# Weight-block sums of two row products, made ahead beside the gate and up products and kept in DRAM

## The chip, the cores and the metric

The kernel runs on one core of a Trainium2 chip. The metric is the device time of one execution in microseconds (us).

## What is computed

One decoder layer on 1024 tokens of width 1024, all in float32. The parts that matter here:

```python
f = _swiglu(_rmsnorm(h, ffn1_pre_g), ffn1_w_gate, ffn1_w_up, ffn1_w_down)
h = h + 0.5 * _rmsnorm(f, ffn1_post_g)
z = _rmsnorm(h, mix_pre_g) @ w_in            # u | v | pool | gate a | gate b
...                                          # gated spatial and pooling mixers, projections
f = _swiglu(_rmsnorm(h, ffn2_pre_g), ffn2_w_gate, ffn2_w_up, ffn2_w_down)
h = h + 0.5 * _rmsnorm(f, ffn2_post_g)
gate = jax.nn.sigmoid(_rmsnorm(h, ple_pre_g) @ ple_w_gate)
h = h + _rmsnorm(gate * (p @ ple_w_proj), ple_post_g)
```

The hidden width of both FFNs is 2816.

## The kernel before

Every large product is made by a scheme of seven products of half-size blocks (p1, p2, p5, p6, p3, p7, p4, in this order, `ORDER`). Both operands are needed as blocks and as sums of blocks. Of the left operand (the tokens), class `Seven` keeps seven tiles `X`; of the right operand (the weights), each of the products needs one block or one sum: p1 takes block 11, p2 block 21, p3 block 22; p5 takes 11+12, p6 adds 22 to that, p7 takes 12+22, p4 takes 11+12+22+21. Each float32 operand is then split into a high part (a cast on ScalarE, L147) and the rest (a subtraction on VectorE, L148), and each product of two blocks is three matmuls (`mm3`, L155 to L157).

An FFN first makes the gate and up products (`ffn_hidden`): eleven column groups of seven products with two output tiles each, weights loaded three steps ahead. A finished group is spilled to DRAM with its sums (`spill`), and sums of blocks of the down weights for later are made beside it (`down_sums`, two loads, four sums on VectorE, four stores into `t_d`). Then `ffn_down` makes the down product. Its last step finishes the token tiles 4 to 7 one by one, and `closing` treats each: a square with a sum on ScalarE (L168), a multiplication by the gain (L718), a reciprocal root on GpSimd (L162, L163), the residual on VectorE (L730), again a square (L168) and a root (L162, L163), and the scaling of the normalised tile (L178, into a `raw` tile). TensorE transposes that tile (L232), and `feed` turns it into the left operands of the next product (L148, L207, L212 to L215). I call the time of these four tiles the passage.

Behind each passage stands a row product (class `Rows`: seven steps, four output tiles each): v after the first FFN, the gate of the layer's end after the second. TensorE meanwhile makes p1 and p2 of it, two tile products between one transpose and the next. Its weights are made one step ahead. Those of v and of the last gate are built from the blocks as they are needed (`from_blocks`): loads at L522, and for p5, p6, p7 and p4 sums on VectorE (`each`, L151), two of 128x1024 per step, on tiles of the pool `raw`, which has six buffers. The blocks 11, 12 and 22 stay in these buffers until p7 has used them. The same pool holds the residual input of each token tile (L725) and, at the end, the output tiles (L1185). The row product by `w_o` has its sums from DRAM already (`from_stored`).

Small pieces of work are queued in `Later` with a key (the lowest goes first) and a cost in us; after each tile product some credit is given and pieces are let out. A timeline model then orders the instructions of each engine, and each engine, SP with its DMA queue too, runs them strictly in that order. The pools are `raw` (6), `f` (11 tiles of 128x1024), `hf` (4 of 128x512) and PSUM (8 banks).

Of the kernel before, what the change touches and what calls it, by code (L numbers as in the profile page):

```python
# [13 lines left out]
P = 128  # L14
T = 1024
D = 1024
# [5 lines left out]
HT = 512  # L22
# [61 lines left out]
def layer_kernel(ctx: ExitStack, tc: tile.TileContext, a: dict, out: bass.AP):  # L84
    nc = tc.nc
    x, p = a["x"][0], a["p"][0, 0]
# [13 lines left out]
    later = Later()  # L100
# [4 lines left out]
    def wt(shape):  # L105

        return wtp.tile([P, *shape], FR, name="wt", tag="wt")

    def raw(shape, dt=F32):

        return rawp.tile([P, *shape], dt, name="raw", tag="raw")

    def full(shape=(D,), dt=F32):

        return fp.tile([P, *shape], dt, name="f", tag="f")
# [11 lines left out]
    def scratch(name, n, w=D):  # L127
        return [dr.tile([P, w], F32, name=f"{name}{i}", tag=f"{name}{i}") for i in range(n)]
# [3 lines left out]
    ga_d, gb_d, y_d = (dr.tile([P, KD, T], F32, name=s, tag=s) for s in ("ga_d", "gb_d", "y_d"))  # L132
    as_d, bs_d = (scratch(s, 7, KD // 2 * HT) for s in ("a_s", "b_s"))

    tw_d = {s: [scratch(f"{s}_t{h}", 4) for h in range(2)] for s in ("w_out_a", "w_out_b", "w_o")}
    ws_d = dr.tile([P, HT], F32, name="ws_d", tag="ws_d")
    sv_d = dr.tile([P, KD, T], F32, name="sv_d", tag="sv_d")
# [12 lines left out]
    def add(dst, u, v, e=nc.vector):  # L150
        e.tensor_tensor(dst, u, v, op=ALU.add)  # L151
# [37 lines left out]
    class Seven:  # L189
        def __init__(self):  # L190
            self.op, self.kept = [None] * 7, {}
            count[0] += 10
            self.base = count[0]
# [10 lines left out]
        def sums(self, k, cols, a11, a12, a21, a22, s1, us):  # L204


            nc.vector.tensor_tensor(s1, a22, a21, op=ALU.subtract)  # L207
            self.put(2, k, cols, s1)
            self.put(6, k, cols, a22)

            def others():
                nc.vector.scalar_tensor_tensor(s1, a11, -1.0, s1, op0=ALU.mult, op1=ALU.subtract)  # L212
                self.put(3, k, cols, s1)
                nc.vector.scalar_tensor_tensor(a12, a12, -1.0, s1, op0=ALU.mult, op1=ALU.subtract)
                nc.vector.tensor_tensor(a11, a11, a21, op=ALU.subtract)  # L215

            later.before(self.base + 3, 4 * us, others)
            later.before(self.base + 4, us, lambda: self.put(4, k, cols, a12))
            later.before(self.base + 5, us, lambda: self.put(5, k, cols, a11))
# [145 lines left out]
    def from_blocks(block, put):  # L365


        def each(u, v):
            for x, y in zip(u, v):
                add(x, x, y, nc.vector)  # L370

        def make(i, st, keep):
            name = ORDER[i][0]
            if name in ("p1", "p2"):
                b = block(i, 0)
                if keep[i]:
                    st[("11", "21")[i]] = b
                return put(b)
            if name == "p5":
                st["11"] = st.get("11") or block(0, 0)  # L380
                st["12"] = block(0, 1)
                each(st["11"], st["12"])
                return put(st["11"])
            if name == "p6":
                st["22"] = block(1, 1)
                each(st["11"], st["22"])
                return put(st["11"])
            if name == "p3":
                return put(st["22"])
            if name == "p7":  # L390
                each(st["12"], st["22"])
                return put(st["12"])
            each(st["11"], st.get("21") or block(1, 0))
            return put(st["11"])

        return make

    def from_stored(block, put, sums):


        def make(i, st, keep):
            where = {"p1": (0, 0), "p2": (1, 0), "p3": (1, 1)}
            name = ORDER[i][0]
            return put(block(*where[name]) if name in where else sums(("p5", "p6", "p7", "p4").index(name)))

        return make
# [97 lines left out]
        return [one(t) for t in range(4)]  # L504

    class Rows:
        def __init__(self, w, stored=None):

            state = {}

            def sums(j):
                out = [raw([2, HT]) for _ in range(2)]
                for h, t in enumerate(out):
                    nc.sync.dma_start(t, stored[h][j].rearrange("p (k f) -> p k f", k=2))
                return out

            def block(r, c):
                out = []
                for h in range(2):
                    t = raw([2, HT])  # L520
                    r0 = r * HT + h * 256
                    nc.sync.dma_start(t, w[r0:r0 + 256, c * HT:(c + 1) * HT].rearrange("(k p) f -> p k f", p=P))  # L522
                    out.append(t)
                return out

            def put(b):
                out = []
                for h in range(2):
                    o = wt([2, 2, HT])
                    split(o[:, 0], o[:, 1], b[h])  # L530
                    out.append(o)
                return out

            make = from_stored(block, put, sums) if stored else from_blocks(block, put)
            self.right = Right(lambda i: make(i, state, (False, False)), list(range(7)), 1)

        def run(self, left, outs, last):
# [21 lines left out]
    def spill(g, dst):  # L559


        def keep(i, src):
            nc.sync.dma_start(dst(i), src)

        def first():
            keep(0, g["11"])
            keep(1, g["12"])
            keep(6, g["22"])
            s1, s2 = half(), half()
            nc.vector.tensor_tensor(s1, g["22"], g["21"], op=ALU.subtract)  # L570
            keep(2, s1)
            nc.vector.scalar_tensor_tensor(s2, g["11"], -1.0, s1, op0=ALU.mult, op1=ALU.subtract)
            keep(3, s2)
            g["s2"] = s2

        def second():
            s3, s4 = half(), half()
            nc.vector.scalar_tensor_tensor(s4, g["12"], -1.0, g["s2"], op0=ALU.mult, op1=ALU.subtract)
            keep(4, s4)
            nc.vector.tensor_tensor(s3, g["11"], g["21"], op=ALU.subtract)  # L580
            keep(5, s3)

        later.add(0, 1.4, first)
        later.add(0, 1.4, second)
# [3 lines left out]
        wg, wu = (a[f"{s}_w_{n}"][0] for n in ("gate", "up"))  # L588
        return Columns(HC, lambda c: ((wg, c, c + HC), (wu, c, c + HC)), 2)

    def ffn_hidden(s, left, cols, last):
        wd = a[f"{s}_w_down"][0]
        hid = {}

        def down_sums(c):

            state = []

            def put(i, u, v):
                o = half()  # L600
                add(o, u, v)
                nc.sync.dma_start(t_d[s][i][:, c * HT:(c + 1) * HT], o)
                return o

            def first():
                w = []
                for b in range(2):
                    w.append(full((2, HT)))
                    r = (c + b * HC) * P
                    nc.sync.dma_start(w[b], wd[r:r + P, :].rearrange("p (j f) -> p j f", j=2))  # L610
                b11, b12, b21, b22 = (w[i][:, j, :] for i in range(2) for j in range(2))
                t2 = put(3, put(2, b11, b12), b22)
                state.append(lambda: (put(6, t2, b21), put(5, b12, b22)))

            later.add(90, 1.4, first)
            later.add(91, 1.4, lambda: state.pop()())

        def outs(c):
            g = hid[c] = {}
            _, places, others = packed()  # L620

            def gate(key, src):
                g[key] = places(key)
                nc.scalar.activation(g[key], src, AF.Silu)

            def up(key, src):
                nc.vector.tensor_tensor(g[key], g[key], src, op=ALU.mult)

            return [Out(gate, places), Out(up, others)]

        def after(c):
            spill(hid.pop(c), lambda i: s_d[s][i][:, c * HT:(c + 1) * HT])
            if c < HC - 1:
                down_sums(c)
            if c == HC - 2:
                down_sums(c + 1)
            if c == HC - 1:
                later.flush()

        cols.run(left, outs, after, lambda i: last() if i == 6 else None)  # L640
# [108 lines left out]
    w_in = a["w_in"][0]  # L749
    h1_cols = hidden_weights("ffn1")  # L750
# [53 lines left out]
    left = Seven()  # L804
# [66 lines left out]
        return steps  # L871

    down = down_weights("ffn1")
    ffn_hidden("ffn1", left, h1_cols, lambda: down.ahead(3))
    v_rows = Rows(w_in[:, D:2 * D])
    left = Seven()
    ffn_down(
        down, closing(4.0, lambda t: x[t * P:(t + 1) * P, :], h1_d, "ffn1_post_g", "mix_pre_g", left),
# [6 lines left out]
    v, sgu = {}, []  # L885
# [264 lines left out]
    h2_cols = hidden_weights("ffn2")  # L1150
    left = Seven()
# [3 lines left out]
    )  # L1155

    down = down_weights("ffn2")
    ffn_hidden("ffn2", left, h2_cols, lambda: down.ahead(3))
    ple_rows = Rows(a["ple_w_gate"][0])
    left = Seven()  # L1160
    ffn_down(
        down, closing(4.0, lambda t: h2_d[t], h3_d, "ffn2_post_g", "ple_pre_g", left),
# [60 lines left out]
```

## Time and profile before

| what | before |
|---|---|
| median of three runs | 2148.37 us (2146.13 to 2148.41) |
| the profiled execution | 2153.78 us |
| its span | 2151.7 us |
| TensorE busy | 2070.9 us (96%) |
| VectorE busy | 1472.0 us (68%) |
| ScalarE busy | 939.9 us (44%) |
| moved by DMA | 429.52 MB, mean 200 GB/s |

Times in the profile count from the span's start. The gate and up products of the first FFN lie at about 60 to 480 us, its passage at 690 to 730; those of the second FFN at 1440 to 1830, its passage at 2030 to 2070. The last gate's product follows to the end.

### The profile page before, as it was taken

How to read it: one execution, taken by the hardware profiler on the slowest of the kernel's cores; microseconds unless marked ns; L12 is line 12 of the kernel's file. 1: busy time of each engine (PE TensorE's matmuls, PEld its weight loads, DVE VectorE, ACT ScalarE, POOL GpSimd, SP SyncE). 2: the span in 40 equal slices, each digit the busy share in tenths (PEclk: the TensorE clock that was granted, in tenths of full speed). 3: DMA queues.
4: the chain of work that ended last, by engine and by line, in shares of the span. 5: the costliest groups of instructions: out<-in, count | busy, mean ns of one | idle time of the engine just before them, and what ended most of it. 6: DMA issues, size and time to landing. Idle time of an engine off the chain costs nothing. (4 is left out here: it accounts for less than half of the span.)

```text
span 2151.7 us, 25497 instructions
## 1 busy us (share of the span) xinstructions
PE 2070.9 (96%) x9228; PEld 1712.7 (80%) x9228; DVE 1472.0 (68%) x1773; ACT 939.9 (44%) x1360; POOL 141.0 (7%) x212
## 2 busy tenths in 40 slices
PE   7999999999999799999999999989999999999986
PEld 6888888888887688888787887778888888888765
DVE  6866666677566887567576758886666667545687
ACT  7533333344435543334455535643333334444553
POOL 2000000000021110000000002300000000002112
PEclk9999999999999899999999999999999999999988
DMA  8454545399768236445389986635454547764635
GB/s 287 128 171 157 176 142 184 129 340 384 298 221 320 69 100 193 158 142 177 128 282 340 324 233 204 195 112 188 146 186 136 172 149 272 231 197 175 225 118 195
DMA packets 301486, 429.52 MB, mean 200 GB/s; under 512 B 19888, under 2 KB 176560, under 8 KB 301360
## 3 DMA queue, kind: packets, MB, share of 16 engines
q1 hardware_dynamic: 300272, 425.80, 58.3%
q0 software_dynamic: 1088, 2.10, 0.6%
q8 instruction: 72, 1.18, 0.2%
q14 instruction: 54, 0.44, 0.1%
HBM read 290.72 MB, written 137.10 MB: 199 GB/s over the span
## 5 line engine op out<-in xcount | busy, mean ns | idle before, releaser
L155 PE MATMUL ps<-X,wt 128*128 128x512 f32 x1904 | 743.0, 391 | 4.1 <-DVE f L345 2.4
L156 PE MATMUL ps<-X,wt 128*128 128x512 f32 x1904 | 743.2, 390 | 0.9 <-DVE X L148 0.9
L157 PE MATMUL ps<-X,wt 128*128 128x512 f32 x1904 | 741.8, 390 | 0.0
L148 DVE TENSOR_TENSOR wt<-raw,wt 128x1024 fp32r<-128x1024 f32 x282 | 343.5, 1220 | 235.0 <-ACT wt L147 234.9
L155 PEld LDWEIGHTS ps<-X,wt 128*128 128x128 f32 x1904 | 359.3, 189 | 79.3 <-DVE f L345 2.8
L156 PEld LDWEIGHTS ps<-X,wt 128*128 128x128 f32 x1904 | 359.2, 189 | 76.0 <-DVE X L148 1.8
L157 PEld LDWEIGHTS ps<-X,wt 128*128 128x128 f32 x1904 | 358.8, 188 | 74.7
L147 ACT CAST wt<-raw 128x1024 fp32r<-128x1024 f32 x282 | 295.5, 1050 | 268.7 <-PE ps L157 129.2
L148 DVE TENSOR_TENSOR X<-raw,X 128x1024 fp32r<-128x1024 f32 (+1 forms) x201 | 224.0, 1145 | 113.6 <-ACT X L147 113.1
L147 ACT CAST X<-raw 128x1024 fp32r<-128x1024 f32 (+1 forms) x201 | 192.1, 993 | 156.2 <-PE ps L157 66.6
L156 PE MATMUL ps<-X 128*128 128x512 f32 x616 | 241.5, 392 | 0.3 <-DVE X L148 0.3
L155 PE MATMUL ps<-X 128*128 128x512 f32 x616 | 237.4, 391 | 3.7 <-ACT X L147 2.6
L157 PE MATMUL ps<-X 128*128 128x512 f32 x616 | 240.2, 391 | 0.0
L151 DVE TENSOR_TENSOR raw<-raw 128x1024 f32<-128x1024 f32 x136 | 165.8, 1221 | 15.4 <-DMA raw<-in_w_in_dram 5.5
L155 PEld LDWEIGHTS ps<-X 128*128 128x128 f32 x616 | 116.1, 189 | 28.6 <-ACT X L147 3.0
L156 PEld LDWEIGHTS ps<-X 128*128 128x128 f32 x616 | 116.4, 189 | 24.7 <-DVE X L148 0.8
L156 PE MATMUL ps<-wt,X 128*128 128x512 f32 x336 | 133.8, 398 | 1.8 <-DVE wt L148 1.8
L157 PEld LDWEIGHTS ps<-X 128*128 128x128 f32 x616 | 116.4, 189 | 24.0
L155 PE MATMUL ps<-wt,X 128*128 128x512 f32 x336 | 132.1, 401 | 1.2 <-DVE f L345 1.2
L157 PE MATMUL ps<-wt,X 128*128 128x512 f32 x336 | 133.0, 396 | 0.0
L340 ACT ACTIVATE f<-ps 128x512 f32<-128x512 f32 x88 | 52.6, 598 | 122.5 <-PE ps L157 122.3
L338 ACT ACTIVATE f<-ps 128x512 f32<-128x512 f32 x88 | 52.0, 597 | 109.4 <-PE ps L157 109.4
(136 smaller groups left out, 1856.9 us busy)
## 6 DMA issues: line engine op xcount, KB each, us to landing
raw<-ffn_s SPq DMA_DIRECT2D x70, 512.0 KB, 5.2
raw<-in_ffn_w_gate_dram SPq DMA_DIRECT2D x96, 256.0 KB, 3.4
raw<-in_ffn_w_up_dram SPq DMA_DIRECT2D x96, 256.0 KB, 4.1
f<-in_ffn_w_down_dram SPq DMA_DIRECT2D x44, 512.0 KB, 4.6
ffn_s<-hf SPq DMA_DIRECT2D x88, 256.0 KB, 3.4
ffn_t<-hf SPq DMA_DIRECT2D x88, 256.0 KB, 4.3
raw<-ffn_t SPq DMA_DIRECT2D x40, 512.0 KB, 5.2
ffn_s<-f SPq DMA_DIRECT2D x66, 256.0 KB, 2.1
```

What stands on the lines that cost most here:

```text
L147: nc.scalar.copy(hi, src)
L148: e.tensor_tensor(lo, src, hi.bitcast(F32), op=ALU.subtract)
L151: e.tensor_tensor(dst, u, v, op=ALU.add)
L155: nc.tensor.matmul(ps, wl[1], wr[0], start=first, stop=False, skip_group_check=True)
L156: nc.tensor.matmul(ps, wl[0], wr[1], start=False, stop=False, skip_group_check=True)
L157: nc.tensor.matmul(ps, wl[0], wr[0], start=False, stop=last, skip_group_check=True)
L338: nc.scalar.activation(at("22"), y, AF.Copy, scale=-1.0)
L340: nc.scalar.activation(at("12"), x, AF.Copy, scale=-1.0)
```

## The change

`Rows` for v and for the last gate now takes its sums from DRAM, as that for `w_o` did. They are made by a new function, `row_sums`, in four groups per FFN, let out behind the column groups 3 to 6 of the gate and up products: each group loads two tiles of the weights (512 KB each), and, with a wait of two tile products, makes four sums of 128x512 on VectorE and stores them (256 KB each). The keys 92 and 93 stand behind all others.

```diff
+    tr_d = {s: [scratch(f"{s}_t{h}", 4) for h in range(2)] for s in ("w_v", "ple_w_gate")}
...
     class Rows:
-        def __init__(self, w, stored=None):
+        def __init__(self, w, stored):
...
-            make = from_stored(block, put, sums) if stored else from_blocks(block, put)
+            make = from_stored(block, put, sums)
...
+    def row_sums(w, dst):
+        def one(k):
+            tiles = [full((2, HT)) for _ in range(2)]
+            for r, t in enumerate(tiles):
+                rows = w[r * HT + k * P:r * HT + (k + 1) * P, :]
+                nc.sync.dma_start(t, rows.rearrange("p (c f) -> p c f", c=2))
+
+            def sums():
+                b11, b12, b21, b22 = (t[:, c, :] for t in tiles for c in range(2))
+                for d, t, u, v in ((0, b11, b11, b12), (2, b12, b12, b22), (1, b22, b11, b22), (3, b21, b22, b21)):
+                    add(t, u, v)
+                    nc.sync.dma_start(dst[k // 2][d][:, (k % 2) * HT:(k % 2 + 1) * HT], t)
+
+            later.add(93, 2.8, sums, 2)
+
+        return [lambda k=k: later.add(92, 0.0, lambda: one(k)) for k in range(4)]
...
         def after(c):
             spill(hid.pop(c), lambda i: s_d[s][i][:, c * HT:(c + 1) * HT])
+            if c > 2 and beside:
+                beside.pop(0)()
...
-    ffn_hidden("ffn1", left, h1_cols, lambda: down.ahead(3))
-    v_rows = Rows(w_in[:, D:2 * D])
+    ffn_hidden("ffn1", left, h1_cols, lambda: down.ahead(3), row_sums(w_in[:, D:2 * D], tr_d["w_v"]))
+    v_rows = Rows(w_in[:, D:2 * D], tr_d["w_v"])
...
-    ffn_hidden("ffn2", left, h2_cols, lambda: down.ahead(3))
-    ple_rows = Rows(a["ple_w_gate"][0])
+    ffn_hidden("ffn2", left, h2_cols, lambda: down.ahead(3), row_sums(a["ple_w_gate"][0], tr_d["ple_w_gate"]))
+    ple_rows = Rows(a["ple_w_gate"][0], tr_d["ple_w_gate"])
```

The order of the instructions moves with it. First, VectorE in the v passage, from the residual of tile 5 to that of tile 6, before (L730 is the residual, L178 the scaling, L151 on `raw` a sum of weight blocks):

```order
L730 SCALAR_TENSOR_TENSOR f<-f,sc,raw 128x1024
L207 TENSOR_TENSOR X<-ps,X 128x4x128
L151 TENSOR_TENSOR raw<-raw 128x1024
L148 TENSOR_TENSOR X<-X 128x4x128
L178 SCALAR_TENSOR_TENSOR raw<-f,sc 128x1024
L148 TENSOR_TENSOR X<-ps,X 128x4x128
L718 TENSOR_TENSOR f<-ps,f 128x512
L212 SCALAR_TENSOR_TENSOR X<-f,X 128x4x128
L730 SCALAR_TENSOR_TENSOR f<-f,sc,raw 128x1024
```

The same stretch of VectorE in the change, where lines from the transposes on have moved (L753 is the residual, L179 the scaling):

```order
L753 SCALAR_TENSOR_TENSOR f<-f,sc,raw 128x1024
L208 TENSOR_TENSOR X<-ps,X 128x4x128
L149 TENSOR_TENSOR X<-X 128x4x128
L179 SCALAR_TENSOR_TENSOR raw<-f,sc 128x1024
L149 TENSOR_TENSOR X<-ps,X 128x4x128
L213 SCALAR_TENSOR_TENSOR X<-f,X 128x4x128
L741 TENSOR_TENSOR f<-ps,f 128x512
L215 SCALAR_TENSOR_TENSOR f<-f,X 128x512
L216 TENSOR_TENSOR f<-f,X 128x512
L208 TENSOR_TENSOR X<-ps,X 128x4x128
L753 SCALAR_TENSOR_TENSOR f<-f,sc,raw 128x1024
```

The sum ahead of tile 5's scaling is gone, and three operand instructions of tiles 4 and 5 (L215, L216, L208) have moved ahead of tile 6's residual.

Second, VectorE in the same passage from the residual of tile 7 to its scaling, before:

```order
L730 SCALAR_TENSOR_TENSOR f<-f,sc,raw 128x1024
L214 SCALAR_TENSOR_TENSOR f<-f,X 128x512
L215 TENSOR_TENSOR f<-f,X 128x512
L148 TENSOR_TENSOR X<-X 128x4x128
L151 TENSOR_TENSOR raw<-raw 128x1024 x2
L151 TENSOR_TENSOR f<-f,ps 128x512
L148 TENSOR_TENSOR X<-X 128x4x128
L148 TENSOR_TENSOR X<-ps,X 128x4x128
L151 TENSOR_TENSOR f<-f,ps 128x512
L148 TENSOR_TENSOR X<-f,X 128x4x128
L178 SCALAR_TENSOR_TENSOR raw<-f,sc 128x1024
```

And the same stretch in the change:

```order
L753 SCALAR_TENSOR_TENSOR f<-f,sc,raw 128x1024
L149 TENSOR_TENSOR X<-f,X 128x4x128
L152 TENSOR_TENSOR f<-f,ps 128x512
L149 TENSOR_TENSOR X<-X 128x4x128
L149 TENSOR_TENSOR X<-ps,X 128x4x128
L152 TENSOR_TENSOR f<-f,ps 128x512
L213 SCALAR_TENSOR_TENSOR X<-f,X 128x4x128
L936 BN_STATS st<-f 128x6
L179 SCALAR_TENSOR_TENSOR raw<-f,sc 128x1024
```

Two sums and one short instruction fewer stand between the two. What stands ahead of this stretch, from tile 6's scaling on, are eight instructions in both: the scaling, two splits of weights and five short ones.

Third, SP in the gate and up products of the first FFN, in the change, behind column group 3 (`w_v_t` are the stored sums, `ffn_s` and `ffn_t` the spills of the hidden tiles and of the down sums):

```order
L631 DMA f<-in_ffn_w_down_dram 128x1024 x2
L599 DMA f<-in_w_in_dram 128x1024 x2
L564 DMA ffn_s_190<-hf 128x512
L564 DMA ffn_s_191<-hf 128x512
L444 DMA raw<-in_ffn_w_gate_dram 128x4x128
L444 DMA raw<-in_ffn_w_up_dram 128x4x128
L605 DMA w_v_t_146<-f 128x512
L564 DMA ffn_s_192<-hf 128x512
L564 DMA ffn_s_193<-hf 128x512
L444 DMA raw<-in_ffn_w_gate_dram 128x4x128
L444 DMA raw<-in_ffn_w_up_dram 128x4x128
L605 DMA w_v_t_148<-f 128x512
```

The rows L599 and L605 are new; the others stand in the order of before. Each store waits for its sum on VectorE, and the loads behind it on SP wait with it.

## Rows read from the trace of the kernel before

**Rows 1.** The page's busy shares: busy us, share of the span, instructions.

```profile
PE 2070.9 (96%) x9228; PEld 1712.7 (80%) x9228; DVE 1472.0 (68%) x1773; ACT 939.9 (44%) x1360; POOL 141.0 (7%) x212
```

**Rows 2.** Windows, gate and up products: stretch, us, busy by engine, clock, DMA share, GB/s.

```profile
60.00:480.00 420.00, 420.00 (x1855) 347.89 (x1854) 281.35 (x342) 157.88 (x210) 0.00 (x0) 1.00 0.53 177
```

**Rows 3.** Windows of the two passages, same columns.

```profile
692.70:726.40 33.70, 21.26 (x96) 17.16 (x96) 28.79 (x38) 18.30 (x32) 10.60 (x11) 0.88 0.36 117
2034.50:2067.60 33.10, 21.30 (x96) 16.97 (x97) 29.28 (x38) 19.35 (x34) 9.29 (x11) 0.88 0.42 143
```

**Rows 4.** Timeline of TensorE in the v passage: start us, us, instruction, idle before it.

```profile
702.57 1.09 PE L232 MATMUL ps<-ident,raw 128*128 128x128 f32 x8 [3.05 <-DVE raw L178]
...
726.45 1.97 PE L232 MATMUL ps<-ident,raw 128*128 128x128 f32 x8 [6.60 <-DVE raw L178]
```

**Rows 5.** Who waited for whom on TensorE, 690:730 and 2030:2070: total, times, longest.

```profile
PE ps L232 <- DVE raw L178: 12.9, 4, 6.6
...
PE ps L232 <- DVE raw L178: 12.4, 4, 7.2
```

**Rows 6.** Timeline of VectorE in the v passage.

```profile
699.49 1.22 DVE L151 TENSOR_TENSOR raw<-raw 128x1024 f32<-128x1024 f32 x1 [4.10 <-DMA raw<-in_w_in_dram]
...
701.23 1.28 DVE L178 SCALAR_TENSOR_TENSOR raw<-f,sc 128x1024 f32<-128x1024 f32 x1
...
704.22 1.28 DVE L730 SCALAR_TENSOR_TENSOR f<-f,sc,raw 128x1024 f32<-128x1024 f32 x1
...
710.36 1.30 DVE L178 SCALAR_TENSOR_TENSOR raw<-f,sc 128x1024 f32<-128x1024 f32 x1 [0.72 <-POOL sc L163]
...
719.85 2.35 DVE L151 TENSOR_TENSOR raw<-raw 128x1024 f32<-128x1024 f32 x2
...
725.12 1.27 DVE L178 SCALAR_TENSOR_TENSOR raw<-f,sc 128x1024 f32<-128x1024 f32 x1
```

**Rows 7.** Timeline of GpSimd in the v passage.

```profile
696.10 0.19 POOL L162 TENSOR_SCALAR sc<-sc 128x1 f32<-128x1 f32 x1 [2.89 <-ACT raw L168]
696.38 0.55 POOL L163 TENSOR_TENSOR sc<-sc,nhalf 128x1 f32<-128x1 f32 x1
...
706.77 2.92 POOL L162 TENSOR_SCALAR sc<-sc 128x1 f32<-128x1 f32 x1 [8.17 <-ACT raw L168]
...
719.39 2.86 POOL L162 TENSOR_SCALAR sc<-sc 128x1 f32<-128x1 f32 x1 [7.33 <-ACT raw L168]
```

**Rows 8.** Timeline of ScalarE in the v passage.

```profile
695.92 0.60 ACT L147 CAST X<-X 128x512 fp32r<-128x512 f32 x1
```

**Rows 9.** Timeline of VectorE in the passage to the last gate.

```profile
2040.03 1.23 DVE L151 TENSOR_TENSOR raw<-raw 128x1024 f32<-128x1024 f32 x1 [3.02 <-DMA raw<-in_ple_w_gate_dram]
...
2044.77 1.28 DVE L730 SCALAR_TENSOR_TENSOR f<-f,sc,raw 128x1024 f32<-128x1024 f32 x1
...
2050.91 1.30 DVE L178 SCALAR_TENSOR_TENSOR raw<-f,sc 128x1024 f32<-128x1024 f32 x1 [0.72 <-POOL sc L163]
...
2066.27 1.27 DVE L178 SCALAR_TENSOR_TENSOR raw<-f,sc 128x1024 f32<-128x1024 f32 x1
```

**Rows 10.** Timeline of TensorE in p4 of the last product.

```profile
2122.12 0.50 PE L155 MATMUL ps<-wt,X 128*128 128x512 f32 x1 [1.22 <-DVE f L345]
...
2123.26 0.49 PE L156 MATMUL ps<-wt,X 128*128 128x512 f32 x1 [0.63 <-DVE wt L148]
```

**Rows 11.** Timeline of VectorE in the last product and its tail.

```profile
2116.51 1.23 DVE L151 TENSOR_TENSOR raw<-raw 128x1024 f32<-128x1024 f32 x1 [0.48 <-DMA raw<-in_ple_w_gate_dram]
...
2135.25 0.69 DVE L1180 TENSOR_TENSOR f<-f,hf 128x512 f32<-128x512 f32 x1 [3.53 <-DMA hf<-e]
...
2137.13 0.69 DVE L1180 TENSOR_TENSOR f<-f,hf 128x512 f32<-128x512 f32 x1 [1.19 <-DMA hf<-e]
```

**Rows 12.** Instructions of L151 that sum down weights: ns min/median/max, first and last start.

```profile
L151 DVE TENSOR_TENSOR hf<-f x44: 680/683/694, 109.8 to 1810.3; 128x512 f32<-128x512 f32 x44
```

**Rows 13.** DMA issues of the page: count, KB each, median us from issue to landing.

```profile
f<-in_ffn_w_down_dram SPq DMA_DIRECT2D x44, 512.0 KB, 4.6
```

More of the change, by code (lines that the diff above doesn't have):

```diff
@@ L589, in hidden_weights, with ffn_hidden @@
         return Columns(HC, lambda c: ((wg, c, c + HC), (wu, c, c + HC)), 2)
-    def ffn_hidden(s, left, cols, last):
+    def row_sums(w, dst):
[11 more added lines that the diff above has]
+        return [lambda k=k: later.add(92, 0.0, lambda: one(k)) for k in range(4)]
+    def ffn_hidden(s, left, cols, last, beside):
         wd = a[f"{s}_w_down"][0]
```

## The prediction

> **What bounds the kernel now.** I read the busy shares first: TensorE is busy 96% of the span [rows 1], so only its idle stretches can be won, and matmuls are not touched by the change. Windows show where they lie. In the gate and up products TensorE is busy for 420.00 of 420.00 us [rows 2]; there nothing can be won, only lost. In the passage from each FFN into the row product behind it (v, and the last gate), TensorE is busy 21.3 of some 33 us while VectorE is busy 28.8 and 29.3 [rows 3]. The waits in these passages have one form: the transposes of a normalised token tile (L232) wait for L178, the scaling on VectorE. In the v passage the longest are 3.05 and 6.60 us [rows 4]; four of them make 12.9 us there, and 12.4 in the gate's passage [rows 5]. In VectorE's timeline the reader is to see why L178 is late. Ahead of tile 5 VectorE stands still for 4.10 us before a sum of weight blocks (L151) whose block is still on its way, and L178 of tile 5 stands behind it at 701.23; tile 6 follows at 710.36, and tile 7 at 725.12, with two more sums (2.35 us) in between [rows 6]. The reciprocal root that tile 5 needs was ready on GpSimd at 696.93, long before [rows 7]. The gate's passage has the same pattern with a stand of 3.02 us [rows 9].
>
> **The change, part by part.** I cost it on the profiled execution (span 2151.7, whole 2153.8 us), which lies 5.4 us above the median of the three runs (2148.4); I take the difference off the median.
>
> *Sums in the gate and up products: 0.* Each FFN gets four groups of two loads, four sums and four stores: 16 sums of 0.683 us [rows 12] make 10.9 us on VectorE over four columns, and 4 MB in plus 4 MB out. VectorE is busy 281 of 420 us there and the DMA share is 0.53 [rows 2]; 8.4 MB over four columns (about 152 us, 55 GB/s, beside 177) raise it to about 0.7. What hides them is TensorE, which looks three steps ahead in its weights. Were nothing hidden, the two FFNs would lose 2 x 10.9 = 21.8 us; below 0 a gain is excluded, as TensorE has no idle time there. I take 0, for the 44 sums of 0.683 us that already run there cost TensorE nothing. On SP the four stores of a group stand among the spills and weight loads, each behind its own sum.
>
> *Loads of the row products: 0.* Twelve block tiles become six plus eight stored sums, 14 of 512 KB. But sum, partner and spare block no longer sit in the six `raw` buffers: a step holds two, where p5 to p4 held up to six. The sums for p5 are queued on SP right behind the four residual tiles, ahead of the stores of the residual, and wait only for the buffers of p1 and p2.
>
> *The passages: 5.3 us each.* The eight sums of each product go, four of them in the passage. Tile 5 first: VectorE needs the residual of tile 5, a subtraction, a split of X whose cast ends on ScalarE at 696.52 [rows 8], and the root of 696.93 [rows 7]. So L178 of tile 5 can run at about 697.15, 4.1 us earlier than 701.23; in the gate's passage the 3.02 us of the stand [rows 9]. Then the new order costs something: between this scaling and the residual of tile 6 it has six short instructions in place of three. How long is a short one? From L178 of tile 6 to that of tile 7 VectorE runs without a pause for 14.76 us: 6 instructions of 1024 columns at 1.175 (half of the 2.35 of the two sums [rows 6]), and 13 short ones, which leaves 0.593 each. So three more are 1.8 us, and the residual of tile 6 starts 4.1 - 1.8 = 2.3 us earlier (v) and 3.0 - 1.8 = 1.2 (gate). From there to L178 of tile 6 it took 704.22 to 710.36, 6.14 us, in the gate's passage 2044.77 to 2050.91, the same; I keep 6.14. From tile 6 to tile 7 the order now has 4 long and 12 short ones in v: 11.8 in place of 14.76, 3.0 less. In the gate's passage it has 4 and 11: 11.2 in place of 15.36, 4.1 less [rows 9]. Together 2.3 + 3.0 = 5.3 and 1.2 + 4.1 = 5.3 us. TensorE's own work between the transposes is unchanged and shorter than this, so the transposes of tile 7, and everything after them, come 5.3 us earlier in each. The waits do not vanish: of some 12 us there remain about 7 each. The low level of the clock that follows the long wait (0.88 on average over each passage [rows 3]) I leave in. Bounds: 2.35 us each, if only the two sums ahead of tile 7 go and all else is late for other reasons; 12.4 each, if all the waits go.
>
> Here one assumption weighs. In the 6.14 us lies a GpSimd step that took 2.92 us at 706.77, and 2.86 at 719.39, while VectorE ran without a pause; each ended when VectorE's run of sums and splits did (722.25 against 722.20 for the second). With VectorE at rest at 696.10 it took 0.19 [rows 6, 7]. The Trainium skill (SBUF — State Buffer, Who interferes with whom) says that a VectorE instruction with two SBUF inputs contends with a GpSimd instruction that reads SBUF, and that one with at most one SBUF input does not. These rows agree. The new order puts a split with a PSUM input among the others earlier, which by that rule lets GpSimd in sooner; what this would give is a rival below.
>
> *The last product: 1.9 us.* The sum for p4 waits until an output tile frees its buffers and its block lands, and TensorE then waits 1.22 us for a read of VectorE and 0.63 for the split of these weights [rows 10]. The stored sums of p4 are queued ahead of all output stores, and their buffers come free with p7's split. I take all of the 1.9; the bounds are 0 and 1.9.
>
> *The tail behind the last matmul: 4.7 us.* VectorE waits there 3.53 and 1.19 us for tiles of e [rows 11]. The `hf` buffers of these come free as p7's tiles are squared, which stood behind the two p4 sums (one of them 1.23 us at 2116.51, after a wait of its own for the block) [rows 11]. Bounds: 0, if the e tiles stay as late relative to TensorE; 7.1, if both sums (2.35) and both waits (4.7) go. I take the waits alone, 4.7, the row that measures what is late.
>
> **Sum**: 5.3 + 5.3 + 1.9 + 4.7 = 17.2 us, so 2148.4 - 17.2 = **2131.2 us** (2136.6 against the profiled execution).
>
> **The rivals.** *GpSimd gets in sooner.* With the step at 0.2 in place of 2.9 us, but with three casts and a copy put ahead of the square on ScalarE in the new order, I get some 5.1 in place of 6.14: 1.0 less in each passage, 2129.1. Speaks for it: the row at 696.10. Against: the new order too runs VectorE almost without a pause. By the rule of the page cited above this is what happens.
> *All waits go*: 12.9 + 12.4 in the passages, 1.9 and 4.7: 31.9 us, 2116.5. It needs each L178 to be ready before TensorE arrives; the chain of residual, square, root and scaling speaks against it.
> *The chain, not the sums*: VectorE's work is only regrouped, and each passage gains no more than its two sums: 2.35 + 2.35 + 1.9 = 6.6, 2141.8. For it: six short instructions now stand where three stood.
> *It does not do it*: a split of p5's weights now stands between tiles 6 and 7 on VectorE and waits for a cast that waits for TensorE to end p1; if that costs the 5.3 again and the tail keeps its lateness, only 1.9 remains: 2146.5.
> *Slower*: in the gate and up products a new sum waits on VectorE for its load (a load of this size lands after 4.6 us in the median [rows 13]); splits of weights and reads of PSUM queue behind it, and so do SP's next weight loads behind the store. If TensorE loses a whole landing in each of the eight groups, it is 36.8 us, less 17.2: 2168.0. It decides from 2.2 us per group. Against it: the sums for the down product load in the same manner, and TensorE's 420.00 of 420.00 [rows 2] shows no loss.
>
> **How the numbers follow.** Two runs of this kernel can be told apart from about 0.2%, 4.3 us. Chances: the forecast 0.40, GpSimd sooner 0.15, all waits gone 0.12, the chain 0.20: these are faster, 0.87. No change 0.07, slower 0.06. The range reaches from the case where all waits go to the chain's: 2116 to 2143, which leaves out the last two cases (0.13) and a little at both ends.
>
> **What would show it.** Right: no L151 sum on raw tiles in either passage; no wait ahead of the transposes of tile 5; tile 7's wait between 4 and 6 us; no wait of TensorE in p4; 32 sums more in the gate and up products with TensorE still busy without a gap. Wrong: VectorE still pausing for a weight tile in the passage, tile 7's transposes waiting over 6.5 us, or any TensorE wait in the gate and up products. If the passages behave but the time does not, the tail is the term that failed.

## The result and the profile after

The changed kernel takes 2129.42 us (median of four runs, 2127.79 to 2131.33) where the kernel before, run beside it, takes 2147.25 (2146.08 to 2148.41): 17.8 us less, ratio 0.9917, 95% interval 0.9900 to 0.9934 (14.2 to 21.5 us). Forecast were 2131.2 us and 17.2 us less.

| | before | after |
|---|---|---|
| the profiled execution, its span | 2153.78, 2151.7 us | 2130.26, 2128.5 us |
| transposes of tile 4 to those of tile 7, v | 33.49 us | 26.40 us |
| the same, last gate | 33.01 us | 25.90 us |
| last matmul's end to the end | 17.93 us | 14.51 us |

Lines of the kernel after are one higher behind L134, and 23 higher behind the row sums: L148 casts, L149 splits, L152 sums, L179 scales, L233 transposes, L741 and L753 close a tile, L1203 adds e.

The page's busy shares of the kernel after, against [rows 1]: TensorE's 7.9 us less are mostly time at half clock (granted clock 0.50). About half of them belong to that one execution of the kernel before; in a second profile of it (first experiment) TensorE is busy 2066.5 us.

```profile
PE 2063.0 (97%) x9228; PEld 1706.8 (80%) x9228; DVE 1472.5 (69%) x1789; ACT 938.8 (44%) x1360; POOL 141.0 (7%) x212
```

Windows of the kernel after: the gate and up products and the two passages, columns as in [rows 2, 3].

```profile
60.00:480.00 420.00, 420.00 (x1855) 347.89 (x1854) 289.89 (x355) 155.07 (x205) 0.00 (x0) 1.00 0.58 197
692.30:719.00 26.70, 19.50 (x97) 15.88 (x97) 25.44 (x36) 18.52 (x34) 7.36 (x11) 0.97 0.52 187
2024.80:2051.00 26.20, 19.46 (x96) 15.85 (x96) 24.93 (x35) 18.92 (x34) 7.40 (x11) 0.95 0.66 220
```

The products that now carry the sums still have TensorE busy without a gap (420.00 of 420.00); VectorE has 8.5 us more there than in [rows 2], the DMA share went from 0.53 to 0.58. The passages are shorter by 7 us each.

TensorE's waits in the two passages, from its timeline (start us, us, instruction, idle before it): tiles 4, 6 and 7 of v, then tiles 4, 6 and 7 of the last gate. The row of each tile 7 is cut off at the end of its window: it has three of the eight transposes.

```profile
692.57 1.06 PE L233 MATMUL ps<-ident,raw 128*128 128x128 f32 x8 [0.70 <-DVE raw L179]
...
707.11 1.09 PE L233 MATMUL ps<-ident,raw 128*128 128x128 f32 x8 [1.67 <-DVE raw L179]
...
718.97 0.90 PE L233 MATMUL ps<-ident,raw 128*128 128x128 f32 x3 [5.27 <-DVE raw L179]
...
2025.13 1.06 PE L233 MATMUL ps<-ident,raw 128*128 128x128 f32 x8 [0.70 <-DVE raw L179]
...
2039.67 1.09 PE L233 MATMUL ps<-ident,raw 128*128 128x128 f32 x8 [1.65 <-DVE raw L179]
...
2051.03 0.87 PE L233 MATMUL ps<-ident,raw 128*128 128x128 f32 x3 [4.79 <-DVE raw L179]
```

Tile 5 is waited for no longer. The waits make 7.6 and 7.1 us where [rows 5] has 12.9 and 12.4.

VectorE in v's passage, to be laid beside [rows 6]: residual and scaling of tile 5, of tile 6, of tile 7, and a split of a PSUM bank ahead of the second scaling.

```profile
693.11 1.28 DVE L753 SCALAR_TENSOR_TENSOR f<-f,sc,raw 128x1024 f32<-128x1024 f32 x1
...
696.78 1.28 DVE L179 SCALAR_TENSOR_TENSOR raw<-f,sc 128x1024 f32<-128x1024 f32 x1
...
701.58 1.27 DVE L753 SCALAR_TENSOR_TENSOR f<-f,sc,raw 128x1024 f32<-128x1024 f32 x1
...
704.58 0.68 DVE L149 TENSOR_TENSOR X<-ps,X 128x512 fp32r<-128x512 f32 x1
...
705.78 1.27 DVE L179 SCALAR_TENSOR_TENSOR raw<-f,sc 128x1024 f32<-128x1024 f32 x1
...
717.65 1.26 DVE L179 SCALAR_TENSOR_TENSOR raw<-f,sc 128x1024 f32<-128x1024 f32 x1
```

GpSimd under it, against [rows 7]: the root's first step for tile 6, and the first step of tile 7's residual root.

```profile
704.53 0.19 POOL L163 TENSOR_SCALAR sc<-sc 128x1 f32<-128x1 f32 x1 [5.71 <-ACT raw L169]
...
706.07 2.25 POOL L163 TENSOR_SCALAR sc<-sc 128x1 f32<-128x1 f32 x1 [0.72 <-ACT hf L169]
```

From the residual of tile 6 to its scaling it is now 4.20 us (701.58 to 705.78); it was 6.14. GpSimd's step that took 2.92 us [rows 7] takes 0.19: it falls beside the split from PSUM. From the scaling of tile 6 to that of tile 7 it is 11.87 us; it was 14.76, and 11.8 were forecast.

The tail, in three fences: the last matmul of the kernel after, VectorE's only wait for a tile of e near it, and the last matmul of the kernel before.

```profile
2113.60 0.39 PE L158 MATMUL ps<-wt,X 128*128 128x512 f32 x1
```

```profile
2112.98 0.72 DVE L1203 TENSOR_TENSOR f<-f,hf 128x512 f32<-128x512 f32 x1 [2.29 <-DMA hf<-e]
```

```profile
2133.38 0.39 PE L157 MATMUL ps<-wt,X 128*128 128x512 f32 x1
```

The wait for e is over at 2112.98, 1.0 us before the last matmul ends; before, VectorE waited until 2137.13 [rows 11], 3.4 us behind it. In p4 of the last product TensorE no longer waits (1.22 and 0.63 us in [rows 10]).

### The profile page after: what moved, and what is told of

The parts are those of the page before. It is cut to its first block, busy times and chain, and to the rows that moved or that the text cites. A ratio compares the mean times of both kernels' runs of the same rounds, so it can differ in the third digit from the quotient of the medians.

```text
span 2128.5 us, 25640 instructions
## 1 busy us (share of the span) xinstructions
PE 2063.0 (97%) x9228; PEld 1706.8 (80%) x9228; DVE 1472.5 (69%) x1789; ACT 938.8 (44%) x1360; POOL 141.0 (7%) x212
## 5 line engine op out<-in xcount | busy, mean ns | idle before, releaser
L149 DVE TENSOR_TENSOR wt<-raw,wt 128x1024 fp32r<-128x1024 f32 x282 | 343.9, 1221 | 227.2 <-ACT wt L148 222.4
L148 ACT CAST wt<-raw 128x1024 fp32r<-128x1024 f32 x282 | 295.6, 1049 | 262.6 <-PE ps L158 121.2
L149 DVE TENSOR_TENSOR X<-raw,X 128x1024 fp32r<-128x1024 f32 (+1 forms) x201 | 223.8, 1145 | 108.7 <-ACT X L148 108.1
L148 ACT CAST X<-raw 128x1024 fp32r<-128x1024 f32 (+1 forms) x201 | 192.0, 993 | 152.3 <-PE ps L158 75.7
L152 DVE TENSOR_TENSOR raw<-raw 128x1024 f32<-128x1024 f32 x120 | 146.6, 1222 | 7.7 <-DMA raw<-in_ffn_w_up_dram 3.5
```

The costliest lines, as they stand in the source:

```text
L148: nc.scalar.copy(hi, src)
L149: e.tensor_tensor(lo, src, hi.bitcast(F32), op=ALU.subtract)
```

## The experiments

Each was timed beside the kernel before on the same chip; differences are of medians. The kernel before had medians of 2145.46 to 2147.25 us beside the different runs, so the difference between two of the changed kernels is uncertain by some 2 us; where it matters I give it both ways, from the times and from the column "against before". "Passage" in the table is the time from the transposes of tile 4 to those of tile 7, from each run's profile.

| run | us | against before | ratio (95%) | passage v, gate |
|---|---|---|---|---|
| before again | 2146.49 | 0.0 | 0.9998 (0.9989 to 1.0007) | 33.20, 33.01 |
| v's sums alone | 2143.18 | -3.3 | 0.9983 (0.9975 to 0.9992) | 26.41, 32.73 |
| gate's sums alone | 2133.90 | -12.6 | 0.9943 (0.9930 to 0.9956) | 33.06, 25.92 |
| sums made, not read | 2147.83 | +1.3 | 1.0009 (1.0000 to 1.0018) | 33.39, 32.64 |
| after, VectorE's time put back | 2142.39 | -3.7 | 0.9980 (0.9972 to 0.9989) | 32.23, 31.58 |
| after, other sums held back | 2112.58 | -33.5 | 0.9845 (0.9832 to 0.9858) | 19.06, 19.08 |
| before, other sums held back | 2142.68 | -3.4 | 0.9988 (0.9977 to 0.9998) | 27.35, 26.95 |
| after, TensorE kept busy | 2124.49 | -21.0 | 0.9900 (0.9883 to 0.9916) | 26.40, 26.41 |
| other sums held back, gate's sums alone | 2125.22 | -20.2 | 0.9904 (0.9890 to 0.9919) | 29.21, 19.21 |

**The kernel before once more**, for a second profile and the scatter.

> The kernel before, unchanged, profiled a second time. Theory A: its first profiled execution was 5.4 us above the median of its runs because of chance (late transfers of e at the end, one wait of 6.2 us in the u and pooling product); the ratio is 1.000 and this profile's span comes nearer to 2145. Theory B: these waits belong to the kernel; then the span is again about 2150 and the last matmul again about 18 us ahead of the end.

The time came out the same. Its profile has waits of 12.6 and 12.5 us in the passages. It also shows what was chance in the first one: the tail was 16.00 us, not 17.93, as VectorE waited less for the first tile of e (3.53 us in [rows 11]):

```profile
2127.91 0.69 DVE L1180 TENSOR_TENSOR f<-f,hf 128x512 f32<-128x512 f32 x1 [1.65 <-DMA hf<-e]
2129.79 0.69 DVE L1180 TENSOR_TENSOR f<-f,hf 128x512 f32<-128x512 f32 x1 [1.19 <-DMA hf<-e]
```

Of the wait of 6.2 us that the expectation names, TensorE's rows of the first profile show 2.39 us (at 1131.82), and 0.22 us at the same place in this one.

**v's sums alone.** The second FFN makes no sums, the last gate reads blocks.

```diff
-    ffn_hidden("ffn2", ..., row_sums(a["ple_w_gate"][0], tr_d["ple_w_gate"]))
-    ple_rows = Rows(a["ple_w_gate"][0], tr_d["ple_w_gate"])
+    ffn_hidden("ffn2", ..., [])
+    ple_rows = Rows(a["ple_w_gate"][0])
```

> Stored sums for v alone; the last gate builds its sums as before. Theory A (each passage gains by itself, some 7.1 us as the changed kernel's trace shows): 2147.3 - 7.1 = 2140 us, and the transposes of tile 7 in the v passage wait 5.3 us, in the other passage 7.2 as before. Rival B (the halves gain from each other, or the order elsewhere in the middle of the kernel gives another 3 us): 2137 or less, with a shorter stretch between the two passages. Rival C (the end is where the gain lies): 2145 or more.

**The gate's sums alone**, the same edit on the other FFN.

```diff
-    ffn_hidden("ffn1", ..., row_sums(w_in[:, D:2 * D], tr_d["w_v"]))
-    v_rows = Rows(w_in[:, D:2 * D], tr_d["w_v"])
+    ffn_hidden("ffn1", ..., [])
+    v_rows = Rows(w_in[:, D:2 * D])
```

> Stored sums for the last gate alone; v builds its sums as before. Theory A: the passage gives 7.1 us and the last product with its tail the rest of the 17.8 us measured, 17.8 - 14.2 = 3.6: 2147.3 - 10.7 = 2136.6 us. Rival B (the tail gives what I forecast for it, 1.9 + 4.7): 2147.3 - 7.1 - 6.6 = 2133.6. Rival C (nothing in the tail): 2140.

Each half shortens its own passage by 7 us and leaves the other. The gate's half gave 12.6 us: the 7.1 of its passage (33.01 to 25.92), 1.7 of the tail (16.00 to 14.30), 1.3 of p4, where the second profile of before has 0.66 and 0.63 us of waits and this one none, and 2.5 that these rows do not hold (some 0.8 of it is less work at half clock behind tile 7). v's half gave 3.3 (the interval reaches from 1.7 to 5.4), less than its passage; the section on the prediction comes back to this. The two make 15.9, within their intervals of the 17.8.

**Sums made and stored, not read**: both products go back to blocks, the sums in the FFNs stay.

```diff
-    v_rows = Rows(w_in[:, D:2 * D], tr_d["w_v"])
+    v_rows = Rows(w_in[:, D:2 * D])
...
-    ple_rows = Rows(a["ple_w_gate"][0], tr_d["ple_w_gate"])
+    ple_rows = Rows(a["ple_w_gate"][0])
```

> The sums are made and stored beside the gate and up products of both FFNs, but not read: v and the last gate build theirs as before. Theory A (hidden by TensorE): within 0.1% of the kernel before, 2147 us, TensorE busy without a gap in the gate and up products. Rival B (they cost and the gain in the passages is larger than the difference shows): each of the eight groups costs up to 2 us, 2150 to 2163.

Making them costs 1.3 us, with an interval of 0 to 3.9, and TensorE is busy for 420.00 of 420.00 us in the gate and up products here too. So no wait there, and at most a small price elsewhere.

**VectorE's time put back.** Is it the time of the sums on VectorE, or their standing for late blocks? In the changed kernel each loaded stored sum gets one more operation of the sum's size.

```diff
             def sums(j):
                 out = [raw([2, HT]) for _ in range(2)]
                 for h, t in enumerate(out):
                     nc.sync.dma_start(...)
+                    if again:
+                        nc.vector.tensor_tensor(t, t, t, op=ALU.max)
```

> The changed kernel with one VectorE operation added on each of the 16 loaded stored-sum tiles (an in-place maximum of the tile with itself, two inputs in SBUF, 128x1024, about 1.2 us like the sum that it stands for; the values stay as they are). The loads stay 2 MB each and come early as in the changed kernel; only VectorE's time and its reads of SBUF are put back. Theory A (the sums cost by VectorE's time, 8 operations of 1.2 us in each of the two passages, and by GpSimd's waits under them): most of the gain goes: tile 7's transposes stand about 6 to 7 us later in each passage, the wait for tile 7 is back at 7 us or more, and the time is 2140 to 2145 us, 0.996 to 0.999 of the kernel before. Rival B (the sums cost by standing in VectorE's stream for blocks that land late and by holding the raw buffers): the extra operations find their data there and fit into VectorE's pauses; the time stays within 3 us of the changed kernel's 2129.4 us, and tile 7's wait stays near 5.3 us.

Theory A. 13.0 of the 17.8 us are gone again (14.1 by the column): the passages are 5.8 and 5.7 us longer than in the changed kernel, the tail 1.7 (16.19 us). TensorE in v's passage, who waited for whom (total, times, longest):

```profile
PE ps L233 <- DVE raw L179: 11.8, 4, 7.0
```

In v's passage one of these operations stood 0.76 us for its load, and one behind the passage 1.45; nothing else there waited for data. In the gate's passage one stood 2.72 us:

```profile
2034.85 1.23 DVE L517 TENSOR_TENSOR raw<-raw 128x1024 f32<-128x1024 f32 x1 [2.72 <-DMA raw<-ple_w_gate_t]
```

So in v's passage VectorE's time is most of what the change saves in this order of work. In the gate's passage a late load is up to half of the 5.7 us, and the run does not separate the two there.

**The other sums held back.** What is left of the wait for tile 7 should be VectorE's queue. The sums of the token tiles for p6, p3 and p7 (L213 to L216 and their splits), which only the fourth product and later ones need (the expectation says the fifth), are put behind the scaling of tile 7 in both passages; `issue_after` sets an order and computes nothing.

```diff
     def others():
-        nc.vector.scalar_tensor_tensor(s1, a11, -1.0, s1, op0=ALU.mult, op1=ALU.subtract)
+        with tc.issue_after(self.hold) if self.hold else nullcontext(): nc.vector.scalar_tensor_tensor(s1, a11, -1.0, s1, op0=ALU.mult, op1=ALU.subtract)
...
     def norm():
-        scaled(hp, ft, state["r"], g_pre)
+        left.hold = (scaled(hp, ft, state["r"], g_pre), None)[0].ins if t == 7 and factor == 4.0 else (scaled(hp, ft, state["r"], g_pre), None)[1]
...
```

> The changed kernel with one order added: in the two passages the third to fifth sums of the token tiles (needed only from the fifth product on) are queued on VectorE behind the scaling of tile 7. Nothing is computed otherwise. Theory A (what is left of tile 7's wait, 5.3 us in v's passage and 4.8 in the last gate's, is VectorE's queue: between the residual of tile 6 and the scaling of tile 7 it runs 11 such operations of 0.6 us): tile 7 comes 4 to 6 us sooner in each passage, the wait for it goes to under 1 us, and the time is 2119 to 2123 us, 0.987 to 0.989 of the kernel before. Rival B (tile 7 is held by the chain of ScalarE's squares and GpSimd's roots, which run on whatever VectorE does): tile 7's wait falls by less than 2 us in each passage, and the time is 2126 to 2129 us. Rival C (the sums that are put off are late for the fifth product): a wait opens ahead of the fifth product in each passage, and the time is at or above the changed kernel's 2129.4 us.

More than theory A said: 2112.58 us, 16.8 below the changed kernel (15.7 by the column). All that TensorE still waits for in v's passage, and the same in the gate's:

```profile
PE ps L156 <- ACT X L249: 1.0, 1, 1.0
PE ps L233 <- DVE raw L179: 0.7, 1, 0.7
```

VectorE from the scaling of tile 6 to that of tile 7: 7.05 us, where the changed kernel has 11.87.

```profile
703.79 1.28 DVE L179 SCALAR_TENSOR_TENSOR raw<-f,sc 128x1024 f32<-128x1024 f32 x1
...
707.31 1.28 DVE L753 SCALAR_TENSOR_TENSOR f<-f,sc,raw 128x1024 f32<-128x1024 f32 x1
...
710.84 1.28 DVE L179 SCALAR_TENSOR_TENSOR raw<-f,sc 128x1024 f32<-128x1024 f32 x1
```

The waits fell by 11.4 us in both passages together (14.8 to 3.4). The expectation counted these; most of the other 5.4 came from the clock, as the run with TensorE kept busy shows below.

**The same order in the kernel before**, the same edit, with the weight sums made in the passages.

> The kernel before with the same order alone: the third to fifth sums of the token tiles behind the scaling of tile 7, and the weight sums still made in the passage. Theory A (both changes take work from the same queue in the same wait; in the kernel before tile 7's wait is 8.1 us in the second profile of it, of which 6 to 7 us are such operations): tile 7's wait falls by about 5 us in each passage, and the time is 2135 to 2139 us, 0.994 to 0.996 of the kernel before; the stored sums then bring the rest. Rival B (blocks of weights that land late hold VectorE's stream, whatever is put off behind them): tile 7's wait falls by less than 2 us and the time is 2143 to 2147 us.

Only 3.4 us, at the edge of B's numbers, though tile 7's wait fell from 8.1 to 4.1 us, nearly as A said. VectorE in v's passage, then who waited for whom on TensorE:

```profile
698.61 1.23 DVE L151 TENSOR_TENSOR raw<-raw 128x1024 f32<-128x1024 f32 x1 [3.46 <-DMA raw<-in_w_in_dram]
...
706.37 1.23 DVE L151 TENSOR_TENSOR raw<-raw 128x1024 f32<-128x1024 f32 x1 [1.56 <-DMA raw<-in_w_in_dram]
...
730.06 2.35 DVE L151 TENSOR_TENSOR raw<-raw 128x1024 f32<-128x1024 f32 x2
```

```profile
PE ps L232 <- DVE raw L178: 8.4, 4, 4.1
PE ps L155 <- DVE f L151: 2.1, 1, 2.1
```

The passage does shorten by 6 us, but VectorE stands 3.46 and 1.56 us for two blocks on the way and makes four sums of 1.2 us, and a new wait of 2.1 us (2.4 in the gate's passage) opens behind it, with half clock after it. That wait is for VectorE, which has the put-off sums and two more weight sums (2.35 us) ahead of the read that TensorE waits for. So what is left with this order is the weight sums; how much of that is their late blocks and how much their time on VectorE, no run separates. The order alone gives 3.4 us, the change alone 17.8, both together 33.5.

**TensorE kept busy** ahead of tile 7's transposes, with 20 matmuls into a bank that these overwrite.

```diff
                 for q in range(2):
                     ps = bank()
+                    for j in range(-self.busy if t == 7 and q == 0 else 0, 4): nc.tensor.matmul(ps, self.op[0][:, 0, 0, 0:P], self.op[1][:, 0, 0, :], start=True, stop=True, skip_group_check=True) if j < 0 else None
...
+        left.busy = 20 if factor == 4.0 else 0
```

> The changed kernel with 20 matmuls put on TensorE ahead of the transposes of tile 7, in each of the two passages. They write a PSUM bank that the transposes then overwrite, so nothing is computed otherwise; at the 0.23 us between matmuls that the trace shows at full clock they fill about 4.6 us of the waits for tile 7 (5.26 and 4.79 us), in which TensorE now stands. Theory A (TensorE's granted clock falls to 0.50 because it stands in that wait, and the first 5 us of work behind it run at half speed, which costs 2.6 us in v's passage and 2.2 in the last gate's): the clock stays at 1.00 behind the transposes of tile 7, tile 7 itself comes when it did, and the time falls by 4 to 5 us to 2124 to 2126 us. Rival B (the half clock has another cause, or the extra matmuls hold tile 7's transposes up): the windows behind tile 7 still show 0.50, or the transposes stand later by what the matmuls take, and the time is 2128 to 2132 us.

Theory A, in the clock and in the time. Windows behind tile 7 (stretch, us, TensorE busy, granted clock, DMA share, GB/s), first of the changed kernel, then of this one:

```profile
718.00:720.00 2.00, 1.03 (x5) 0.50 0.01 3
720.00:722.00 2.00, 2.00 (x8) 0.50 0.48 105
722.00:724.00 2.00, 2.00 (x6) 0.50 0.72 189
```

```profile
718.00:720.00 2.00, 1.79 (x12) 1.00 0.10 26
720.00:722.00 2.00, 2.00 (x10) 1.00 0.64 119
722.00:724.00 2.00, 2.00 (x11) 1.00 0.63 253
```

Tile 7 comes no sooner (26.40 and 26.41 us after tile 4, where the changed kernel has 26.40 and 25.90), and the kernel is 4.9 us faster (3.1 by the column). In the changed kernel 5.0 us of work run at 0.50 in these rows, the lower of the clock's two levels (1.2 against 2.4 GHz), which loses 2.5; behind tile 7 of the gate's passage it is 4.3 us of work, which loses 2.2 in the same way.

**Other sums held back, the gate's weight sums alone stored**: what is v's half worth once VectorE's queue is out of the way?

> The third to fifth sums of the token tiles behind the scaling of tile 7 in both passages, as in the run of 2112.6 us, but only the last gate's weight sums are made early and stored; v's are made in its passage as in the kernel before. Theory A (with VectorE's queue out of the way v's passage is bound by blocks of weights that land late, so v's half of the change is worth more here than without that order): the passage of v stands and runs as in the kernel before with the order alone (10.4 us of waits and 3.4 us lost at half clock, against 1.7 and 0), less some 2 us that making v's sums costs; the time is 2121 to 2125 us, so v's half is worth 9 to 12 us. Rival B (v's half is worth what it was without the order, 3.3 us): 2115 to 2117 us.

Theory A, just past its range: 2125.22 us, so v's half is worth 12.6 us there (13.3 by the column), against 3.3 without that order. In v's passage TensorE waits much as in the kernel before with that order, and VectorE stands 3.77 and 3.12 us for two blocks:

```profile
PE ps L233 <- DVE raw L179: 7.5, 3, 4.0
PE ps L156 <- DVE f L152: 2.1, 1, 2.1
```

## Why the prediction was right, and where its terms were off

The total came within 2 us, and most of its steps are seen in the rows; two terms were mis-sized, in opposite directions, so that the total came so near is in part luck. The rival *GpSimd gets in sooner* named 2129.1 us, which is nearer to the measured 2129.42 than the forecast; the interval does not tell the two apart.

*Sums in the gate and up products: 0.* Right. TensorE has no gap there in any run, and making the sums costs 1.3 us (0 to 3.9). The rival that ended slower is out.

*The passages: 5.3 us each.* They gave 7.1 each (33.49 to 26.40, 33.01 to 25.90). Step by step in v: this profile's passage begins 0.39 us sooner (692.57 for 692.96), which I add back. The scaling of tile 5 was forecast for 697.15 and comes at 697.17; the residual of tile 6 for 701.92 (704.22 less 2.3), and it comes at 701.97. The last part, from the scaling of tile 6 to that of tile 7, took 11.87 us for 11.8. The gate's passage shows the same (11.27 us from tile 6 to tile 7, for 11.2). The step that failed is the one in between, "I keep 6.14": it took 4.20 in both passages. Two things made the 1.9 us. The rival *GpSimd gets in sooner* happened; in the kernel before its root came 0.72 us after VectorE was ready [rows 6], and now VectorE does not wait for it. The casts that I put ahead of the square on ScalarE cost at most 0.44 us (the residual ends at 702.85, the square starts at 703.29). The other 1.2 us the forecast left in: one of the four weight sums of the passage stood in this very stretch, and went with the others.

```profile
707.83 1.21 DVE L151 TENSOR_TENSOR raw<-raw 128x1024 f32<-128x1024 f32 x1
```

The Trainium skill (SBUF — State Buffer, Who interferes with whom) says that a VectorE instruction with two SBUF inputs contends with a GpSimd instruction that reads SBUF. The traces agree for most of these steps: 0.19 us beside a split from PSUM, and 2.25 us for the first step of the next root at 706.07, which ended (708.32) just after VectorE began an instruction with a PSUM input (L741, 708.12). One does not fit: in the kernel before with the other order such a step ended while VectorE ran a scaling (0.76 us at 707.57).

Why did the waits nevertheless fall by just 5.3 us in each passage, as forecast? In the first profile of before TensorE ran its work between tiles 6 and 7 partly at half clock (3.3 us of it in v's passage) and came to tile 7 that much later; now it is there sooner and waits for what VectorE has not won. Windows of the kernel before, then after:

```profile
712.00:714.00 2.00, 2.00 (x10) 0.50 0.00 0
```

```profile
708.00:710.00 2.00, 2.00 (x11) 1.00 0.31 52
```

The lesson is that the change of a wait is not the change of time where TensorE's own speed between two waits changes; the start of the transposes is.

"The low level of the clock ... I leave in" was right for this change: behind tile 7 it stays (0.50 in the rows above), as the wait of 5.3 us stays. But it was not sized, and 4.9 us (3.1 by the column) lay in it.

*All waits go* did not happen with this change, but the reason that I gave against it (the chain of residual, square, root and scaling) was wrong: with the other sums out of VectorE's queue the same chain leaves 1.7 us of waits in each passage. VectorE's order was the bound, not the chain.

*The last product: 1.9 us.* The waits of p4 are gone; the second profile of before had 1.3 of them.

*The tail: 4.7 us.* Too large. I took both waits for e of one execution; the second profile has 1.65 us where the first has 3.53, and after the change one wait of 2.29 is left, which ends ahead of the last matmul's end. From the last matmul to the end it was 17.93 and 16.00 us before and is 14.51: 1.5 to 3.4 us.

*Sum*: 7.1 + 7.1 + (1.3 to 1.9) + (1.5 to 3.4) - 1.3 for making the sums is 15.7 to 18.2; measured 17.8. What the passages gave more, the tail gave less.

What v's half lacks: alone it measured 3.3 us where its passage gave 6.8 to 7.1. In its profile the transposes of v's tile 7 come 6.8 us before those of the second profile of before (718.68 against 725.47), and those of the gate's tile 4 only 4.7 before (2025.43 against 2030.09), so 2.1 us are given back between the passages. Two waits of TensorE there hold them:

```profile
804.72 0.33 PE L156 MATMUL ps<-f,raw 128*128 128x128 f32 x1 [0.90 <-DVE raw L945]
1124.17 0.50 PE L156 MATMUL ps<-X,wt 128*128 128x512 f32 x1 [1.51 <-DVE f L346]
```

The first is a price of the change: the changed kernel (0.84 us), this run and the run with TensorE kept busy (0.70) have it, and no run with v's sums made in the passage has it; nor have those with v's sums stored and the other sums held back, or VectorE's time put back. The second is chance: the two profiles of before have 2.39 and 0.22 us there. Making the sums costs something as well (1.3 us for both products), and the profiled execution of this run was the fastest of its eleven (2140.72, median 2143.18). Why the others took longer is open.

## What to carry to other kernels

Moving work out of a bound stretch is worth what the next bound leaves: here the weight sums and the other sums stood in VectorE's queue ahead of one wait; taking out the first gave 17.8 us alone, putting off the second 3.4, and both together 33.5. Before pricing a wait, list what the engine it waits for does ahead of the waited instruction, and ask which of it is needed only later; an ordering edge that computes nothing differently gave, on top of the change, about as much as the change itself. And take a price from more than one profiled execution where it hangs on a DMA's landing: the tail's 3.53 us was chance.

## What the runs showed of the hardware

The granted clock adds to a long wait of TensorE: behind the waits of 5.27 and 4.79 us some 5 and 4 us of work ran at 0.50, and 20 useless matmuls in each wait gave 4.9 us back (3.1 by the column). The length of one wait does not tell it alone: in the first profile of before the wait of 3.05 us ahead of tile 5 [rows 4] was followed by full clock and the 2.58 us ahead of tile 6 by half clock; in the second the 2.78 us ahead of tile 5 was followed by half clock. Windows behind tile 5, of the first profile, then of the second:

```profile
704.00:706.00 2.00, 2.00 (x10) 1.00 0.61 115
```

```profile
704.00:706.00 2.00, 2.00 (x6) 0.50 0.80 287
```

The Trainium skill (TensorE: Matmul & The Clock Gate, HAM oscillation) describes such a fall after idle stretches; the run with the matmuls agrees.
